# Blocks of 128-token and 64-token experts in turns, fifth place at 64 tokens, largest expert's rest at 32

## The chip, the cores and the metric

The kernel runs on one core of a Trainium2 chip, in one launch. The metric is the device time of one execution in microseconds (us), taken as the median of several runs. TensorE multiplies matrices into PSUM, ScalarE (ACT) and VectorE (DVE) work on tiles, SyncE (SP) issues nearly all transfers from HBM to SBUF, and GpSimd (POOL) does a few small things.

## The reference

Two layers. Each mixes 256 tokens of width 1024 (an RWKV-7 group, an attention group and a gated-MLP group) and then applies a SwiGLU feed-forward: a dense one in layer 0, and in layer 1 the best two of eight experts for each token.

```python
def swiglu(h, wg, wu, wd):
    return (jax.nn.silu(h @ wg) * (h @ wu)) @ wd

def moe_swiglu(h, router, wg, wu, wd):
    t = h.reshape(B_ * S_, D_)                      # 256 x 1024
    logits = (t @ router).astype(jnp.float32)
    top_v, top_i = lax.top_k(logits, TOP_K)         # 2 of 8
    gates = jax.nn.softmax(top_v, axis=-1)
    gate_full = jnp.sum(jax.nn.one_hot(top_i, N_EXPERTS) * gates[..., None], axis=1)
    out = jnp.zeros_like(t)
    for e in range(N_EXPERTS):                      # wg, wu: 1024 x 3584, wd: 3584 x 1024
        out = out + gate_full[:, e:e + 1] * swiglu(t, wg[e], wu[e], wd[e])
    return out
```

All is float32. The change is in the experts alone.

## The kernel before

**Places.** The experts' stage gathers each expert's tokens and computes on those. Expert 0 has place 0; the other seven are sorted by their token count at run time into places 1 (most tokens) to 7. A place has a fixed number of tokens (`KINDS`, `PLACES`, `CAPS`): 128 for places 0, 2, 3 and 4 (wide), 64 for places 5, 6 and 7 (narrow), 128 and a rest of 64 for place 1. If an expert had more tokens than its place, `rest` would compute those at the end, under a condition read at run time, and load the expert's weights again.

**Blocks.** The 3584 hidden columns are cut into seven blocks of 512 (`NB`). A block needs 4 MB of gate and up weights and 2 MB of down weights: six loads of 1 MB (`eload`, lines 1106 and 1108, issued by SP in the order of use) into 12 buffers named raw, which are handed out in turn. Each load is two halves of 1024 columns.

**Wide products.** For 128 tokens a half is split into two reduced-precision parts wh and wl (`split`: ScalarE line 189, VectorE line 190), and each product is three fast ones (`mm3`, lines 194 to 196). A wide block is 72 products of 512 columns: 48 up (into pb), 24 down (into pa). Splits are put two halves ahead of their use (`AHEAD`), into three buffers plus one.

**Narrow products.** For 64 tokens the raw half is used in full precision and not split. The weights' columns are cut in two, and the two products write PSUM rows 0 to 63 and 64 to 127 (`HALF`), so that they use different column halves of the array (line 1437 up, 32 a block; line 1491 down, 8 a block). The profile has two records for each full-precision product.

**Between them.** `gate_up` ends in silu (ScalarE, line 1446) and the product of gate and up (VectorE, line 1449); `act_T` transposes the result (lines 1467 and 1461) and copies it to aT (lines 1470 and 1463); `do_down` multiplies it with the down weights one block later.

**Order.** `SEQUENCE` says which blocks follow each other: places 0, 3 and 2 whole; then pieces of place 1 (two, three and two blocks) with places 7, 6 and 5 whole between them; place 4 last. Place 1's rest goes with its wide blocks and uses the same weights. `halves` supplies the loads and splits in that order; `take` and `fill` keep three halves at hand. `prepare` gathers a place's tokens (lines 1240 and 1254) and `finish` scales an expert's result and adds it back to x (lines 1360, 1361, 1379, 1380); both are cut into steps that are put between the products (`step`). A place that comes in several parts is finished after each part. What comes out is then put in a final order on each engine by a scheduler, so that products of different tiles can stand between each other.

```python
SEQUENCE = ((0, 0, 7), (3, 0, 7), (2, 0, 7), (1, 0, 2), (7, 0, 7), (1, 2, 5), (6, 0, 7), (1, 5, 7), (5, 0, 7), (4, 0, 7))
CAPS = [sum(PLACES[k] for k in KINDS[p]) for p in range(NE)]
```

## Time and profile before

| | us |
|---|---|
| median of 3 runs | 1571.8 (1570.5 to 1573.4) |
| profiled execution, its own time | 1577.0 |
| its span, first to last instruction | 1575.1 |
| span up to the experts' first weight product | 556.5 |

The mean granted TensorE clock is 0.978 of full speed. A row of the timeline gives start and length, engine, line, operation and tiles, out<-in; xN merges N rows of one kind. A row of a group ends in busy time and the mean length in ns, then the engine's idle time just before such instructions and what ended it. A row of a window gives the stretch, its length, the busy time of TensorE, its weight loads, VectorE, ScalarE and GpSimd (with their instructions), the granted clock, the DMA engines' busy share and GB/s. Lengths of products overlap, so the distance of two starts says more than a length.

### The profile page before, as it was taken

What the parts mean: (1) busy time and instruction counts of PE and PEld (TensorE: products, weight loads), DVE (VectorE), ACT (ScalarE), POOL (GpSimd) and SP (SyncE); (2) the same over time, 40 slices, a digit from 0 to 9 for tenths busy, and PEclk for the clock granted to TensorE, in tenths of its full rate; (3) what the DMA queues carried; (4) which work ended last, traced back from release to release, by engine and by line L of the source; (5) the groups of instructions that cost most, each with busy time, mean ns of one, the idle gap of its engine ahead of it and who ended that gap; (6) DMA issues with size and microseconds to landing.
All of it is one profiled execution on the core that took longest, in us unless ns stands there. A gap on an engine that the chain in (4) does not pass through costs nothing.

```text
span 1575.1 us, 24008 instructions
## 1 busy us (share of the span) xinstructions
PE 1530.2 (97%) x9448; PEld 1133.3 (72%) x9448; DVE 941.9 (60%) x1246; ACT 822.9 (52%) x1166; POOL 79.2 (5%) x127
## 2 busy tenths in 40 slices
PE   8988999999988999999999999999999999999997
PEld 7977788888968788888888876555555555555775
DVE  5775654556774578898898876312542044204886
ACT  7565544446555467777777764203341034114774
POOL 1320000001320100000000000000000000000000
PEclk9999999999987889999999999999999999999999
DMA  6500455553514369998998975799848997899990
GB/s 254 186 29 6 183 187 187 187 177 132 186 55 164 118 249 365 369 352 329 370 368 310 360 294 191 272 411 427 354 169 331 425 427 279 336 400 427 426 411 30
DMA packets 59865, 422.57 MB, mean 268 GB/s; under 512 B 7136, under 2 KB 7136, under 8 KB 9824
## 3 DMA queue, kind: packets, MB, share of 16 engines
q1 hardware_dynamic: 59184, 420.03, 69.1%
q8 instruction: 76, 1.25, 0.3%
q10 hardware_dynamic: 560, 0.93, 0.2%
q14 instruction: 45, 0.37, 0.1%
HBM read 419.88 MB, written 1.05 MB: 267 GB/s over the span
## 4 chain that ended last, share of the span: by engine, by line
PE 83%; DMA 3%; DVE 3%; ACT 3%; POOL 2%; issue 1%; ACTq 0%; SPq 0%
PE pb L1437 12%; PE pb L194 11%; PE pb L195 11%; PE pb L196 11%; PE pa L194 7%; PE pa L195 7%; PE pa L196 7%; PE pa L1491 5%; DMA raw<-moe 3%; PE pb L1254 1%; PE pb L1467 1%; PE pb L1240 1%; PE pb L731 1%; POOL rq_y L202 1%; ACT area L964 1%
## 5 line engine op out<-in xcount | busy, mean ns | idle before, releaser
L190 DVE TENSOR_TENSOR wl<-raw,wh 128x1024 fp32r<-128x1024 f32 (+1 forms) x538 | 642.0, 1220 | 246.4 <-ACT wh L189 240.6
L189 ACT ACTIVATE wh<-raw 128x1024 fp32r<-128x1024 f32 (+1 forms) x538 | 559.6, 1055 | 342.9 <-PE pb L196 160.3
L194 PE MATMUL pb<-wh,xg 128*128 128x512 f32 x560 | 226.4, 405 | 1.7 <-ACT wh L189 1.5
L1437 PE MATMUL pb<-raw,xgs 128*64 128x256 f32 x1792 | 227.0, 384 | 0.0
L195 PE MATMUL pb<-wl,xg 128*128 128x512 f32 x560 | 225.7, 403 | 0.3
L196 PE MATMUL pb<-wh,xg 128*128 128x512 f32 x560 | 221.8, 396 | 0.0
L1437 PEld LDWEIGHTS pb<-raw,xgs 128*64 128x64 f32 x1792 | 125.4, 136 | 87.9 <-issue 34.2
L1449 DVE SCALAR_TENSOR_TENSOR a<-pb,rg,a 128x512 f32<-128x512 f32 (+1 forms) x63 | 39.5, 629 | 161.1 <-PE pb L1437 147.8
L194 PEld LDWEIGHTS pb<-wh,xg 128*128 128x128 f32 x560 | 105.9, 189 | 38.9 <-issue 10.0
L195 PEld LDWEIGHTS pb<-wl,xg 128*128 128x128 f32 x560 | 106.1, 189 | 31.4 <-issue 5.8
L196 PEld LDWEIGHTS pb<-wh,xg 128*128 128x128 f32 x560 | 105.9, 189 | 23.1 <-issue 0.5
L1446 ACT ACTIVATE a<-pb,rg 128x512 f32<-128x512 f32 (+1 forms) x63 | 37.3, 593 | 162.2 <-PE pb L1437 137.8
L195 PE MATMUL pa<-wl,aT 128*128 128x512 f32 x280 | 111.6, 399 | 0.0
L196 PE MATMUL pa<-wh,aT 128*128 128x512 f32 x280 | 109.6, 392 | 0.0
L1491 PE MATMUL pa<-raw,aT 128*64 128x512 f32 x448 | 107.8, 599 | 0.0
L194 PE MATMUL pa<-wh,aT 128*128 128x512 f32 x280 | 95.2, 403 | 0.7 <-ACT aT L1470 0.7
L195 PE MATMUL pb<-wl,hTh 128*128 128x512 f32 (+1 forms) x192 | 73.0, 380 | 0.0
L196 PE MATMUL pb<-wh,hTl 128*128 128x512 f32 (+1 forms) x192 | 71.6, 376 | 0.0
L194 PEld LDWEIGHTS pa<-wh,aT 128*128 128x128 f32 x280 | 52.3, 188 | 24.4 <-issue 12.8
L194 PE MATMUL pb<-wh,hTh 128*128 128x512 f32 (+1 forms) x192 | 67.5, 378 | 0.6 <-ACT hTh L277 0.6
L1491 PEld LDWEIGHTS pa<-raw,aT 128*64 128x64 f32 x448 | 30.5, 136 | 48.9 <-issue 45.7
L196 PEld LDWEIGHTS pa<-wh,aT 128*128 128x128 f32 x280 | 52.7, 188 | 10.8
(385 smaller groups left out, 1990.5 us busy)
## 6 DMA issues: line engine op xcount, KB each, us to landing
raw<-moe SPq DMA_DIRECT2D x336, 1024.0 KB, 7.0
raw<-wst SPq DMA_DIRECT2D x54, 1024.0 KB, 4.8
raw<-wst SPq DMA_DIRECT2D x4, 832.0 KB, 5.0
area<-sw_in SPq DMA_DIRECT2D x2, 960.0 KB, 6.7
area<-sw_in SPq DMA_DIRECT2D x2, 664.0 KB, 6.3
x<-x_in SPq DMA_DIRECT2D x2, 512.0 KB, 5.0
raw<-wst SPq DMA_DIRECT2D x2, 512.0 KB, 7.5
out_dram<-x SPq DMA_DIRECT2D x4, 256.0 KB, 3.2
```

The source lines that it names most:

```text
L189: act(h[:, 0:n], t[:, a:b], AF.Copy)
L190: (E or V).tensor_tensor(lo[:, 0:n], t[:, a:b], h[:, 0:n].bitcast(F32), op=ALU.subtract)
L194: T.matmul(o, lhsT=xh, rhs=wh, start=first, stop=False)
L195: T.matmul(o, lhsT=xh, rhs=wl, start=False, stop=False)
L196: T.matmul(o, lhsT=xl, rhs=wh, start=False, stop=last)
L202: G.tensor_tensor(y, m, C("half")[:, 0:n], op=ALU.pow)
L731: T.matmul(ps[HALF[hv], i * 64:(i + 1) * 64], lhsT=lh, rhs=rh, start=(n == 0 and i == 0), stop=(n == len(groups) - 1), skip_group_check=True)
L964: act(s[:, h, :], s[:, h, :], AF.Exp, scale=scale, bias=mx[:, h:h + 1], accum_out=den[:, h:h + 1])
L1437: T.matmul(ps[i][HALF[hv], 0:256], lhsT=z[:, k, :], rhs=w[:, o_:o_ + 256], start=(k == 0), stop=(k == KD - 1))
L1446: act(a[:, 0:m], ps[i][:, 0:m], AF.Silu, scale=r)
L1449: V.scalar_tensor_tensor(res[i][:, 0:m], ps[i][:, 0:m], r, res[i][:, 0:m], op0=ALU.mult, op1=ALU.mult)
L1491: T.matmul(accs[j][0][HALF[nh], :], lhsT=z[:, f, :], rhs=w[:, s_], start=begin, stop=end)
```

## The change

- **Place 4** becomes narrow: 64 tokens in place of 128.
- **Place 1's rest** has 32 tokens in place of 64. Its up and down weights are cut into column quarters: four products of 256 columns write PSUM rows 0 to 31, 32 to 63, 64 to 95 and 96 to 127 (`QUART`, `quarter_up`, `small_down`). They run after the wide block's own products, on the same loads, which stay in their buffers until then.
- **Order.** `SEQUENCE` goes. `work` makes a round for each wide block (places 0, 1, 2, 3 in that order, `WIDES`) and puts one narrow block (places 4, 5, 6, 7, `NARROWS`) into each, none in the first two rounds, two in the 11th and the 20th (`TURNS`). A round is: wide up, quarter up in place 1, wide down of the block before, its quarter down, narrow down of the narrow block before, narrow up.
- **Supply.** `halves` follows the rounds. `fill` counts only split halves, up to two ahead after a `take`, within a window of ten halves.
- **`finish`** has its own buffers (oh, ol) instead of those of the splits, and a form for quarters. Place 1 is finished once.
- **`rest`** computes what exceeds a place in chunks of 64 and 128 tokens.

```diff
-NPT = 4
+NPT = 5
 AHEAD = 2
+WINDOW = 10
...
-WIDE, NARROW = "full", "half"
-PLACES = {WIDE: 128, NARROW: 64}
-KINDS = {0: (WIDE,), 1: (WIDE, NARROW), 2: (WIDE,), 3: (WIDE,), 4: (WIDE,), 5: (NARROW,), 6: (NARROW,), 7: (NARROW,)}
-
-SEQUENCE = ((0, 0, 7), (3, 0, 7), (2, 0, 7), (1, 0, 2), (7, 0, 7), (1, 2, 5), (6, 0, 7), (1, 5, 7), (5, 0, 7), (4, 0, 7))
+WIDE, NARROW, QUARTER = "full", "half", "quarter"
+PLACES = {WIDE: 128, NARROW: 64, QUARTER: 32}
+IOTA = {WIDE: "iota", NARROW: "iota64", QUARTER: "iota32"}
+KINDS = {0: (WIDE,), 1: (WIDE, QUARTER), 2: (WIDE,), 3: (WIDE,), 4: (NARROW,), 5: (NARROW,), 6: (NARROW,), 7: (NARROW,)}
+
+
+WIDES = (0, 1, 2, 3)
+NARROWS = (4, 5, 6, 7)
+
+TURNS = [0, 0] + [2 if _i in (8, 17) else 1 for _i in range(26)]
...
-                    xg.append((kind, late.tile([128, KD, 64], F32, name="xgs", tag="xgs", bufs=3), rs))
+                    w = PLACES[kind]
+                    xg.append((kind, late.tile([128, KD, w], F32, name="xgs", tag="xgs" + kind, bufs=w // 32), rs))
...
+            w = acc[0].shape[-1]
+            parts = (slice(0, 128),) if len(acc) == 2 else HALF if w == 512 else QUART
+            os = []
+            for ps in acc:
+                oh = ap_.tile([128, 512], F32R, name="oh", tag="oh", bufs=2)[:, 0:w]
+                ol = ap_.tile([128, 512], F32R, name="ol", tag="ol", bufs=2)[:, 0:w]
+                act(oh, ps, AF.Identity, scale=sg)
+                V.scalar_tensor_tensor(ol, ps, sg, oh.bitcast(F32), op0=ALU.mult, op1=ALU.subtract)
+                os.append((oh, ol))
...
+            for i in range(DM // w):
+                oh, ol = os[i % len(acc)]
+                rows = parts[i % len(parts)]
+                s_ = slice(i * w, i * w + w)
                 for t in range(2):
-                    ps = pb()
-                    T.matmul(ps, lhsT=pT[:, t * 128:t * 128 + 128], rhs=oh[:, s_], start=True, stop=False)
-                    T.matmul(ps, lhsT=pT[:, t * 128:t * 128 + 128], rhs=ol[:, s_], start=False, stop=True)
+                    ps = pb()[:, 0:w]
+                    lh = pT[rows, t * 128:t * 128 + 128]
+                    T.matmul(ps, lhsT=lh, rhs=oh[rows, :], start=True, stop=False)
+                    T.matmul(ps, lhsT=lh, rhs=ol[rows, :], start=False, stop=True)
...
+        def units(p, i, js):
+            for j in js:
+                r_ = eload(ready[p][0], 6 * i + j)
+                for q in range(2):
+                    a_, b_ = q * 1024, q * 1024 + 1024
+                    if WIDE not in KINDS[p]:
+                        yield None, None, r_[:, a_:b_]
+                    else:
+                        cnt_splits[0] += 1
+                        own = NHL > 0 and cnt_splits[0] % (3 + NHL) < NHL
+                        yield *(split(r_, a_, b_, h2_p, l2_p) if own else split(r_, a_, b_)), r_[:, a_:b_]
+
         def halves():
-            before = None
-            blocks = [(p, i) for p, lo, hi in SEQUENCE for i in range(lo, hi)]
-            for n in range(len(blocks) + 1):
-                for b, js in ((n, range(4)), (n - 1, (4, 5))):
-                    if 0 <= b < len(blocks):
-                        p, i = blocks[b]
-                        whole = KINDS[p] == (NARROW,)
-                        for j in js:
-                            r_ = eload(ready[p][0], 6 * i + j)
-                            for q in range(2):
-                                a_, b_ = q * 1024, q * 1024 + 1024
-                                if whole:
-                                    yield None, None, r_[:, a_:b_]
-                                else:
-                                    cnt_splits[0] += 1
-                                    own = NHL > 0 and cnt_splits[0] % (3 + NHL) < NHL
-                                    yield *(split(r_, a_, b_, h2_p, l2_p) if own else split(r_, a_, b_)), r_[:, a_:b_]
+            m, before = 0, []
+            for n in range(len(wides) + 1):
+                if n < len(wides):
+                    yield from units(*wides[n], range(4))
+                if n > 0:
+                    yield from units(*wides[n - 1], (4, 5))
+                for b in before:
+                    yield from units(*b, (4, 5))
+                before = narrows[m:m + TURNS[n]] if n < len(wides) else []
+                m += len(before)
+                for b in before:
+                    yield from units(*b, range(4))
 
         supply = halves()
         def fill(n=0):
-            while len(feed) <= AHEAD + n:
+            while len(feed) < WINDOW and sum(h[0] is not None for h in feed) <= AHEAD + n:
                 h = next(supply, None)
                 if h is None:
                     break
                 feed.append(h)
 
         def take():
-            fill()
-            return feed.popleft()
-
-        def gate_up(xg, mid):
-            res = []
+            if not feed:
+                fill()
+            h = feed.popleft()
+            fill(-1)
+            return h
...
+        def wide_up(st):
+
+            _, z, rs = st
+            ws = []
+            a = ap_.tile([128, 512], F32, name="a", tag="a0", bufs=2)
             for j in range(2):
-                ps = [pb() for _ in xg]
+                ps = pb()
                 for q in range(4):
                     wh, wl, w = take()
-                    for i, st in enumerate(xg):
-                        for kk in range(2):
-                            k = q * 2 + kk
-                            z = st[1]
-                            if st[0] == WIDE:
-                                s_ = slice(kk * 512, (kk + 1) * 512)
-                                mm3(ps[i], z[:, k, 0, :], z[:, k, 1, :], wh[:, s_], wl[:, s_], k == 0, k == KD - 1)
-                            else:
-                                for hv in range(2):
-                                    o_ = kk * 512 + hv * 256
-                                    T.matmul(ps[i][HALF[hv], 0:256], lhsT=z[:, k, :], rhs=w[:, o_:o_ + 256],
-                                             start=(k == 0), stop=(k == KD - 1))
+                    ws.append(w)
+                    for kk in range(2):
+                        k = q * 2 + kk
+                        s_ = slice(kk * 512, (kk + 1) * 512)
+                        mm3(ps, z[:, k, 0, :], z[:, k, 1, :], wh[:, s_], wl[:, s_], k == 0, k == KD - 1)
...
+        def narrow_up(st):
+
+            _, z, rs = st
+            a = ap_.tile([128, 256], F32, name="a", tag="a1", bufs=2)
+            for j in range(2):
+                ps = pb()[:, 0:256]
+                for q in range(4):
+                    w = take()[2]
+                    for kk in range(2):
+                        k = q * 2 + kk
+                        for hv in range(2):
+                            o_ = kk * 512 + hv * 256
+                            T.matmul(ps[HALF[hv], :], lhsT=z[:, k, :], rhs=w[:, o_:o_ + 256],
+                                     start=(k == 0), stop=(k == KD - 1))
...
+        def quarter_up(st, ws):
+
+            _, z, rs = st
+            a = ap_.tile([128, 256], F32, name="a", tag="a2", bufs=1)
+            ps = pb()[:, 0:256]
+            for k in range(KD):
+                for g in range(4):
+                    o_ = k % 2 * 512 + g % 2 * 256
+                    T.matmul(ps[QUART[g], :], lhsT=z[:, k, :], rhs=ws[g // 2 * 4 + k // 2][:, o_:o_ + 256],
+                             start=(k == 0), stop=(k == KD - 1))
+            act(a[HALF[1], :], ps[HALF[0], :], AF.Silu, scale=rs[1][HALF[0], :])
+            V.scalar_tensor_tensor(a[HALF[1], :], ps[HALF[1], :], rs[1][HALF[1], :], a[HALF[1], :],
+                                   op0=ALU.mult, op1=ALU.mult)
+            return a
...
+        def small_down(acc, kind, i, aT, ws):
+            parts = HALF if kind == NARROW else QUART
+            w = 1024 // len(parts)
+            for f in range(4):
+                for g, rows in enumerate(parts):
+                    T.matmul(acc[rows, :], lhsT=aT[:, f, :], rhs=ws[f][:, g * w:g * w + w],
+                             start=(i == 0 and f == 0), stop=(i == NB - 1 and f == 3))
+
+        def ended(p, kind, acc, final=False):
+
+            (steps.append if final else steps.appendleft)(finish(ready[p][2][KINDS[p].index(kind)], acc, final))
...
+        def work():
+            m, before, wjob = 0, [], None
+            for n in range(len(wides) + 1):
+
+                if wjob is not None:
+                    p, i, a, aq = wjob
+                    aT = wide_T(a)
+                    aqT = small_T(aq, QUARTER, HALF[1]) if aq is not None else None
+                prev, wjob = wjob, None
+                if n < len(wides):
+                    wp, wi = wides[n]
+                    st = ready[wp][1]
+                    a_, ws = wide_up(st[0])
+                    wjob = (wp, wi, a_, quarter_up(st[1], ws) if len(st) > 1 else None)
+                    if wi == 0 and wp != WIDES[-1]:
+                        ask(WIDES[WIDES.index(wp) + 1])
+                    if n == 0:
+                        ask(NARROWS[0])
+                nT = [small_T(a_, NARROW) for _, _, a_ in before]
+                if prev is not None:
+                    ws = wide_down(p, i, aT)
+                    if i == NB - 1:
+                        ended(p, WIDE, accs[p])
+                    if aqT is not None:
+                        if i == 0:
+                            accs[p, QUARTER] = pa()[:, 0:256]
+                        small_down(accs[p, QUARTER], QUARTER, i, aqT, ws)
+                        if i == NB - 1:
+                            ended(p, QUARTER, [accs[p, QUARTER]])
+
+                for (np_, ni, _), z in zip(before, nT):
+                    if ni == 0:
+                        accs[np_] = [pa()]
+                    small_down(accs[np_][0], NARROW, ni, z, [take()[2] for _ in range(4)])
+                    if ni == NB - 1:
+                        ended(np_, NARROW, accs[np_], np_ == NARROWS[-1])
+                new = narrows[m:m + TURNS[n]] if n < len(wides) else []
+                m += len(new)
+                before = []
+                for np_, ni in new:
+                    before.append((np_, ni, narrow_up(ready[np_][1][0])))
+                    if ni == 0 and np_ != NARROWS[-1]:
+                        ask(NARROWS[NARROWS.index(np_) + 1])
...
+                    for kind in (NARROW, WIDE):
+                        if o >= SEQ:
+                            break
+                        here = nc.values_load(over_i[0:1, p:p + 1], min_val=0, max_val=SEQ)
+                        with tc.If(here > o - CAPS[p]):
+                            rest_of(p, kind, o)
```

Three places show what this does to the order. The first is TensorE where narrow and wide blocks meet: pb<-raw,xgs is narrow up, pa<-raw,aT narrow down, pb<-cc,a a transpose, pb<-wh,xg wide up. Before, at the end of the run of place 7:

```order
L1437 MATMUL pb<-raw,xgs 64x256 x24
L1491 MATMUL pa<-raw,aT 64x512 x8
L194 MATMUL pb<-wh,xg 128x512
L1437 MATMUL pb<-raw,xgs 64x256 x8
L1461 MATMUL pb<-cc,a 128x128 x2
L195 MATMUL pb<-wl,xg 128x512
L196 MATMUL pb<-wh,xg 128x512
```

Now, at the end of a round of a late place:

```order
L1531 MATMUL pa<-raw,aT 64x512 x4
L1464 MATMUL pb<-raw,xgs 64x256 x24
L1491 MATMUL pb<-cc,a 128x128 x4
L1464 MATMUL pb<-raw,xgs 64x256 x8
L200 MATMUL pb<-wh,xg 128x512
L201 MATMUL pb<-wl,xg 128x512
L202 MATMUL pb<-wh,xg 128x512
```

Such a change from narrow to wide now comes in every round; the transposes of the wide block before (L1491) stand eight narrow products ahead of the next wide block.

The second is TensorE in place 1. Before, in the block of place 1 that follows place 7 (L1491 here is still place 7's):

```order
L1437 MATMUL pb<-raw,xgs 64x256 x4
L1491 MATMUL pa<-raw,aT 64x512 x8
L194 MATMUL pb<-wh,xg 128x512
L195 MATMUL pb<-wl,xg 128x512
L196 MATMUL pb<-wh,xg 128x512
```

Now, from the end of a wide block's down products to the next wide block (32x256 are the quarters):

```order
L202 MATMUL pa<-wh,aT 128x512
L1531 MATMUL pa<-raw,aT 32x256 x16
L1531 MATMUL pa<-raw,aT 64x512 x8
L1464 MATMUL pb<-raw,xgs 64x256 x32
L1491 MATMUL pb<-cc,a 128x128 x4
L1503 MATMUL pb<-cc,a 128x64 x2
L200 MATMUL pb<-wh,xg 128x512
```

The 16 quarter down products stand together here, with the narrow block behind them and the transposes directly ahead of the wide block; in other rounds of place 1 they are cut by wide products.

The third is ScalarE, where wh<-raw is the first part of a split, a<-pb,rg the silu, and aT<-pb the copy after a transpose (128x4x128 wide, 128x2x2x64 narrow). Before, in a block of place 4:

```order
L189 ACTIVATE wh<-raw 128x1024 x2
L1446 ACTIVATE a<-pb,rg 128x512
L189 ACTIVATE wh<-raw 128x1024 x8
L1470 ACTIVATE aT<-pb 128x4x128
L189 ACTIVATE wh<-raw 128x1024 x4
```

Now, in one round of a late place:

```order
L1494 ACTIVATE aT<-pb 128x4x128
L195 ACTIVATE wh<-raw 128x1024 x7
L1447 ACTIVATE a<-pb,rg 128x512
L195 ACTIVATE wh<-raw 128x1024
L1505 ACTIVATE aT<-pb 128x2x2x64
L195 ACTIVATE wh<-raw 128x1024 x4
L1467 ACTIVATE a<-pb,rg 128x256
```

The copy of the wide aT moved from the middle of the block to its start, behind the narrow silu, and the 12 splits of a block follow it.

221 lines of the change are left out of this document (86 added, 135 removed).

## The prediction

> **What bounds the kernel now.** I read the page's busy shares and its chain of waits first, then windows by stage, then single rows of the experts' stage.
>
> ```profile
> span 1575.1 us, 24008 instructions
> ...
> PE 1530.2 (97%) x9448; PEld 1133.3 (72%) x9448; DVE 941.9 (60%) x1246; ACT 822.9 (52%) x1166; POOL 79.2 (5%) x127
> ...
> PE 83%; DMA 3%; DVE 3%; ACT 3%; POOL 2%; issue 1%; ACTq 0%; SPq 0%
> ```
>
> TensorE is busy 97% of the span and carries 83% of the chain that ended last; transfers carry 3%. So the question is how much TensorE time the change takes out, and whether transfers then become the bound. Only the experts' stage changes. Its first and last weight products are these (timeline, start and length):
>
> ```profile
> 556.53 0.78 PE L194 MATMUL pb<-wh,xg 128*128 128x512 f32 x1
> ...
> 1564.38 0.39 PE L196 MATMUL pa<-wh,aT 128*128 128x512 f32 x1
> ```
>
> The stage is 1564.4 - 556.5 = 1007.9 us. Its unit is a block, 512 hidden columns of one expert. VectorE ends each block's gate and up with one product (L1449), so two of these rows in a steady stretch give the price of a block:
>
> ```profile
> 763.91 0.74 DVE L1449 SCALAR_TENSOR_TENSOR a<-pb,rg,a 128x512 f32<-128x512 f32 x1
> ...
> 815.23 0.74 DVE L1449 SCALAR_TENSOR_TENSOR a<-pb,rg,a 128x512 f32<-128x512 f32 x1
> ...
> 1237.37 0.48 DVE L1449 SCALAR_TENSOR_TENSOR a<-pb,rg,a 128x256 f32<-128x256 f32 x1 [10.38 <-PE pb L1437]
> ...
> 1269.95 0.48 DVE L1449 SCALAR_TENSOR_TENSOR a<-pb,rg,a 128x256 f32<-128x256 f32 x1 [10.38 <-PE pb L1437]
> ...
> 1517.49 0.74 DVE L1449 SCALAR_TENSOR_TENSOR a<-pb,rg,a 128x512 f32<-128x512 f32 x1
> ...
> 1552.82 0.75 DVE L1449 SCALAR_TENSOR_TENSOR a<-pb,rg,a 128x512 f32<-128x512 f32 x1
> ```
>
> Three wide blocks lie between the first two: 51.32 / 3 = **17.11 us**. Three narrow blocks lie between the next two: 32.58 / 3 = **10.86 us**. The last pair, two blocks of place 4, gives 17.67. The program has 35 wide blocks (five places of seven) and 28 narrow ones (21 of places 5 to 7, seven of place 1's rest): 35 x 17.11 + 28 x 10.86 = 598.9 + 304.1 = 903.0 us. The other 104.9 us are gathering, adding back, changes between the two kinds of product, and waits.
>
> Transfers: one block is six loads.
>
> ```profile
> raw<-moe SPq DMA_DIRECT2D x336, 1024.0 KB, 7.0
> ```
>
> ```profile
> 590.00:670.00 80.00, 80.00 (x357) 65.22 (x356) 71.43 (x66) 63.32 (x66) 0.00 (x0) 1.00 0.97 367
> 1085.00:1130.00 45.00, 44.41 (x226) 24.95 (x224) 22.93 (x22) 21.40 (x25) 0.00 (x0) 1.00 1.01 425
> 1445.00:1500.00 55.00, 54.88 (x237) 40.72 (x236) 46.65 (x46) 40.74 (x43) 0.00 (x0) 1.00 1.01 426
> ```
>
> The last three columns are granted clock, DMA share and GB/s. With 12 buffers to refill the queue brings 426 GB/s, while VectorE is 85% busy (46.65 of 55) with splitting. At that rate a block's 6 x 1.0486 MB take 14.8 us: more than a narrow block computes (10.9), less than a wide one (17.1). So a run of seven narrow blocks eats the buffers, and what follows it waits for a while.
>
> **The change, term by term.** Mean splitting costs don't move per block; 84 of 420 splits go, from engines that are not the bound.
>
> *Fifth place, 128 to 64 tokens.* Seven wide blocks go: -7 x 17.11 = **-119.8 us**. Seven narrow blocks come: +7 x 10.86 = +76.0.
>
> *Place 1's rest, 64 to 32 tokens.* Seven narrow blocks go: -76.0, so the narrow count stays 28. Seven quarter blocks come. The chain's pieces of one narrow block price them (start, length, what):
>
> ```profile
> 1226.39 3.43 PE pa L1491 x16
> 1229.83 3.45 PE pb L1437 x32
> 1233.28 0.37 PE pb L1461 x2
> 1233.65 3.60 PE pb L1437 x32
> ```
>
> A full-precision product is two records. Sixteen products of 256 columns take 3.45 us, 0.216 each; eight of 512 take 3.43. That is with the two column halves running together. Whether a quarter product joins three others has no row. From below: four at once, so two pairs' time for four, 0.43. Then 32 up products cost 3.45, 16 down products of 256 columns 1.73, transposes 0.37: 5.5 us a block. From above: no better than two at once, 10.86 us. I count the pieces into which the order of the changed program cuts them, each rounded up to a group of four: 30 pieces up make 69 groups, 17 down 33, so 102 x 0.4315 = 44.0, and with 7 x 0.37 for transposes 46.6 us, 6.7 a block. The row that speaks for this end is the first of these, with its neighbours:
>
> ```profile
> 928.21 0.40 PE L194 MATMUL pb<-wh,xg 128*128 128x512 f32 x1
> 928.54 1.95 PE L1437 MATMUL pb<-raw,xgs 128*64 128x256 f32 x16
> 930.42 0.50 PE L195 MATMUL pa<-wl,aT 128*128 128x512 f32 x1
> ...
> 1099.70 0.39 PE L196 MATMUL pb<-wh,xg 128*128 128x512 f32 x1
> 1100.02 1.08 PE L1437 MATMUL pb<-raw,xgs 128*64 128x256 f32 x6
> 1101.03 0.50 PE L194 MATMUL pb<-wh,xg 128*128 128x512 f32 x1
> 1101.46 0.65 PE L1437 MATMUL pb<-raw,xgs 128*64 128x256 f32 x2
> 1102.04 0.50 PE L195 MATMUL pb<-wl,xg 128*128 128x512 f32 x1
> ```
>
> One product alone holds the array 0.58 us (1101.46 to 1102.04), eight hold it 1.88 (928.54 to 930.42), where eight alone would be 4.6: pairs lose nothing, so groups are independent, and I take **+47 us**.
>
> The Trainium skill, page "TensorE: Matmul & The Clock Gate", Part 3 (Packing small matmuls), measured 3.07 times for four row tiles and 2.38 for three column tiles, not 4 and 3. By it, as an estimate, the 44.0 would be 57, and the total 13 us higher, inside my range; for two halves this trace shows no such loss.
>
> *Interruptions.* In the rows above, entering a narrow piece takes 0.32 where wide products follow each other at 0.23 (763.81 to 764.04 below), and the eight products take 1.88 instead of 8 x 0.216 = 1.73: together 0.25 us a piece. A piece with an odd count also leaves half a group empty (0.2 to 0.4).
>
> ```profile
> 763.81 0.39 PE L195 MATMUL pa<-wl,aT 128*128 128x512 f32 x1
> 764.04 0.39 PE L196 MATMUL pa<-wh,aT 128*128 128x512 f32 x1
> ```
>
> The order has 166 such pieces before (42 odd) and 150 now (47 of them quarters; 20 of the other 103 odd): -16 x 0.25, and 42 x 0.216 against 10 x 0.216 + 10 x 0.43: **-6 us** (0 to -10).
>
> *Adding back and gathering.* Place 1 was finished three times, since its run came in three parts; now once.
>
> ```profile
> L1379 PE MATMUL pb<-oh,pT 128*128 128x512 f32 x28 | 11.9, 442 | 0.3 <-ACT oh L1371 0.3
> ...
> L1380 PE MATMUL pb<-ol,pT 128*128 128x512 f32 x28 | 10.7, 400 | 0.0
> ...
> L1360 PE MATMUL pb<-oh,pT 64*128 64x512 f32 x24 | 9.6, 466 | 0.0
> L1361 PE MATMUL pb<-ol,pT 64*128 64x512 f32 x24 | 8.4, 402 | 0.0
> ```
>
> 104 products become 80 (16 of them half as wide). Between their spacing of wide products (0.23) and busy time per product (11.9 / 28 = 0.43) I take 0.3: **-7 us** (-5 to -10). Gathering (L1254, L1240) stays: one wide turns narrow, a few us at most.
>
> *Waits.* They move both ways. The stages after narrow runs show idle TensorE:
>
> ```profile
> 1432.00:1565.00 133.00, 131.68 (x570) 99.29 (x566) 109.55 (x103) 93.28 (x101) 0.00 (x0) 1.00 0.78 328
> ```
>
> 1.3 us here, 0.6 in the 1085 window, and place 4's 17.67 against 17.11 for its later blocks: some 5 us, hidden waits unseen. Against it, every round now starts a wide block behind a narrow one. In place 4's block the copy of aT stands on ScalarE ahead of the next splits and waits for the transposes; that is the 0.56. In the new order two splits are ahead, and in most rounds the transposes stand eight narrow products (1.7 us) ahead of the wide block's first, which covers the copy; where they stand directly ahead (place 1's rounds) I count 0.56 each. Sum **0** (-12 if waits of the mixed stages were larger than seen, +15 if all 27 rounds pay 0.56).
>
> What is late next? Six loads of a wide and six of a narrow block take 2 x 14.8 = 29.5 us. A round's TensorE time is 17.11 + 10.86 plus a share of the rest, (104.9 - 13) / 28 = 3.3: 31.3 us, in place 1 some 38. So transfers stay just under, and two wide rounds at the start fill the buffers first. SP issues all loads in the order of use. In place 1 four of the 12 buffers stay taken until the quarter products at the block's end, and the loads behind them on SP wait; eight loads then stand ready, 19.7 us of transfer, for the down and narrow products of some 18 us that come first. The two rounds with two narrow blocks need 44.3 us of loads against 42 and draw on 12 buffers.
>
> *Tail.* The last wide place is now added back together with the last narrow one. These rows end the kernel:
>
> ```profile
> 1565.07 1.41 DVE L1372 SCALAR_TENSOR_TENSOR ol<-pa,sg,oh 128x512 fp32r<-128x512 f32 x2 [2.75 <-ACT oh L1371]
> 1566.67 2.48 DVE L1381 TENSOR_TENSOR x<-x,pb 128x512 f32<-128x512 f32 x4 [0.19 <-PE pb L1380]
> ```
>
> Both stand once more, 3.9 us, partly beside the narrow down products (3.43): **+1.5** (0 to +4).
>
> Sum: -119.8 + 47 - 6 - 7 + 0 + 1.5 = -84.3 us. The profiled execution itself took 1577.0 (span 1575.1), so it would be 1492.7; the runs' median is 1571.8, and -84.3 gives **1487 us**. The layers before are re-ordered in a few rows only (and one constant is 64 KB longer): 3 us either way.
>
> **Rivals.**
>
> *Quarters no better than halves.* If both passes of a product must leave before the next group's first, four groups run two at a time: 7 x 10.86 = 76 instead of 47, so 1487 + 29 = 1516. For it: no row has four groups. Against it: in the 928.54 piece eight products take eight times 0.216 plus entry and exit (1.88), with no ninth slot. The Trainium skill, the same page and part, calls products strict FIFO in start and end; by that rule the queue would run this way, and the piece's 1.88 us does not bear it out for two groups.
>
> *Transfers become the bound.* The 590 window has the queue 97% busy at only 367 GB/s while wide blocks run. Were that the most that splitting leaves, 324 loads after the first 12 would take 339.7 MB / 367 = 926 us from 556.5, to 1482; the last narrow block and the tail add about 16: some 1500 as a span, 1497 by the median, up to 1515 with uneven rounds. Against it: the 1445 window, 426 GB/s beside as much splitting; 367 is what 17.11 us blocks ask for (6.29 MB / 17.11 = 368).
>
> *Splits late in every round.* With none ahead, a round would pay copy, split and subtraction, 0.59 + 1.06 + 1.22 = 2.9 us; 27 rounds make 78, so 1565. The durations are those of the rows below.
>
> ```profile
> L190 DVE TENSOR_TENSOR wl<-raw,wh 128x1024 fp32r<-128x1024 f32 (+1 forms) x538 | 642.0, 1220 | 246.4 <-ACT wh L189 240.6
> L189 ACT ACTIVATE wh<-raw 128x1024 fp32r<-128x1024 f32 (+1 forms) x538 | 559.6, 1055 | 342.9 <-PE pb L196 160.3
> ...
> L1470 ACT ACTIVATE aT<-pb 128x512 fp32r<-128x512 f32 x35 | 20.5, 587 | 10.9 <-PE pb L1467 8.4 <-PE pa L196 2.2
> ```
>
> *Slower: the overflow path runs.* From the 65th token of the fifth-fullest place, or the 161st of the fullest, 42 loads and a narrow expert follow alone at the end: 42 x 2.46 = 103 us of loads and some 10 to gather and add: 1600. The reference on its inputs gives 16 tokens to expert 0 and, in order, 147, 120, 70, 55, 54, 36, 14: nine and 13 short of it.
>
> **How the numbers follow.** Forecast 0.68, quarters 0.13, transfers 0.11, late splits 0.05, overflow 0.02, else 0.01. The range: all low bounds together (5.5 a quarter block, -12 waits, -10, -10, no tail) give 1455; they won't all fall together, so 1460. Above, it takes in the first two rivals with the high bound of the waits: 1525. Late splits and overflow stay out. 0.2% (3 us) is what a measurement can tell from no change; faster 0.96, same 0.01, slower 0.03.
>
> **What would show it.** In the changed profile: narrow products in 28 blocks spread over the whole stage, L1449's successors 31 us apart; groups of four 32-column records starting together every 0.216 us; DMA share near 0.95 without long waits of TensorE for loads. Wrong would be: quarter pieces at twice that length, TensorE idle at a round's start by over 1 us, or a DMA rate stuck at 370 with TensorE waiting.

## The result, and the profile after

The changed kernel takes **1525.1 us** (median of 4 runs, 1524.0 to 1528.1), the kernel before on the same chip 1571.2 (1569.1 to 1573.4): ratio 0.971, 95% interval 0.9689 to 0.973. It is faster by 46 us. The forecast was 1487, 84 us faster, and the range ended at 1525: the direction was right, the size was little more than half.

The page of the changed kernel, span, TensorE's busy time, the chain's shares by engine, and one of the costliest groups:

```profile
span 1526.2 us, 23806 instructions
...
PE 1463.4 (96%) x9578; PEld 1056.8 (69%) x9578; DVE 820.5 (54%) x1136; ACT 719.8 (47%) x1073; POOL 80.5 (5%) x127
...
PE 81%; DVE 6%; ACT 3%; POOL 2%; issue 2%; DMA 1%; ACTq 0%; DVEq 0%; POOLq 0%
...
L201 PE MATMUL pb<-wl,xg 128*128 128x512 f32 x448 | 185.4, 414 | 12.9 <-DVE wl L196 12.3
```

Transfers went from 3% to 1% of the chain, so they did not become the bound. VectorE went from 3% to 6%, and the last row says where: TensorE stood idle for 12.9 us ahead of the second product of a wide tile, which reads wl (L201, L195 before), and VectorE's split ended nearly all of it.

The first and last products of the experts' stage (timeline):

```profile
568.72 0.78 PE L200 MATMUL pb<-wh,xg 128*128 128x512 f32 x1
...
1517.58 0.39 PE L1379 MATMUL pb<-ol,pT 64*128 64x512 f32 x1
```

The stage begins 12.2 us later than before (556.5), though nothing was changed ahead of it. From its first weight product to the last product of all, 948.9 us pass where it was 1010.4 (556.5 to 1566.9): 61.5 less. 61.5 - 12.2, and 0.4 more behind the last product, make the 48.9 us between the two spans. (The profiled execution of the kernel before took 1577.0, 5 us over its median, so by the medians, 46.1 us apart, the layers ahead cost some 15.) So there are two questions: why the layers ahead got longer, and what the stage lacks of its 84 us.

Quarters first, since they were the unknown price. Three pieces of quarter products (L1480), with what follows each (timeline):

```profile
776.90 0.62 PE L1480 MATMUL pb<-raw,xgs 128*32 128x256 f32 x2
777.45 0.50 PE L200 MATMUL pb<-wh,xg 128*128 128x512 f32 x1
777.87 0.64 PE L1480 MATMUL pb<-raw,xgs 128*32 128x256 f32 x8
778.44 0.50 PE L201 MATMUL pb<-wl,xg 128*128 128x512 f32 x1
...
813.92 1.91 PE L1480 MATMUL pb<-raw,xgs 128*32 128x256 f32 x26
815.76 0.50 PE L201 MATMUL pb<-wl,xg 128*128 128x512 f32 x1
```

Two records are one product. From the start of a piece to the start of what follows it, one product holds the array for 0.55 us, four for 0.57 and thirteen for 1.84. That is 0.4315 for each group of up to four and 0.12 for the piece: 0.55, 0.55 and 1.85. Two at once, thirteen would need 7 x 0.4315 = 3.02. **Four quarters do run together.** By distance of starts they take 33.6 us up, 16.4 down and 2.0 for transposes: 52.0, or 7.4 a block where 6.7 was forecast.

### The profile page after: what moved, and what is told of

It is laid out like the page before. It is cut to its first block, busy times and chain, and to the rows that moved or that the text cites. A ratio compares the mean times of both kernels' runs of the same rounds, so it can differ in the third digit from the quotient of the medians.

```text
span 1526.2 us, 23806 instructions
## 1 busy us (share of the span) xinstructions
PE 1463.4 (96%) x9578; PEld 1056.8 (69%) x9578; DVE 820.5 (54%) x1136; ACT 719.8 (47%) x1073; POOL 80.5 (5%) x127
## 4 chain that ended last, share of the span: by engine, by line
PE 81%; DVE 6%; ACT 3%; POOL 2%; issue 2%; DMA 1%; ACTq 0%; DVEq 0%; POOLq 0%
PE pb L1464 12%; PE pb L201 10%; PE pb L200 9%; PE pb L202 9%; PE pa L1531 8%; PE pa L201 7%; PE pa L200 6%; PE pa L202 6%; PE pb L1480 2%; DVE wl L196 2%; DMA raw<-moe 1%; PE pb L1262 1%; PE pb L1491 1%; PE pb L1248 1%; POOL rq_y L208 1%
## 5 line engine op out<-in xcount | busy, mean ns | idle before, releaser
L196 DVE TENSOR_TENSOR wl<-raw,wh 128x1024 fp32r<-128x1024 f32 (+1 forms) x454 | 541.6, 1219 | 282.4 <-ACT wh L195 277.3
L195 ACT ACTIVATE wh<-raw 128x1024 fp32r<-128x1024 f32 (+1 forms) x454 | 467.2, 1053 | 276.1 <-PE pb L202 159.6
L201 PE MATMUL pb<-wl,xg 128*128 128x512 f32 x448 | 185.4, 414 | 12.9 <-DVE wl L196 12.3
L200 PE MATMUL pb<-wh,xg 128*128 128x512 f32 x448 | 181.6, 407 | 0.0
L202 PE MATMUL pb<-wh,xg 128*128 128x512 f32 x448 | 177.9, 397 | 0.0
L1531 PE MATMUL pa<-raw,aT 128*64 128x512 f32 (+1 forms) x672 | 128.3, 530 | 0.0
L201 PEld LDWEIGHTS pb<-wl,xg 128*128 128x128 f32 x448 | 85.1, 190 | 49.1 <-DVE wl L196 23.9
L1495 DVE TENSOR_TENSOR aT<-pb,aT 128x512 fp32r<-128x512 f32 x28 | 19.3, 690 | 180.5 <-ACT aT L1494 180.5
L200 PEld LDWEIGHTS pb<-wh,xg 128*128 128x128 f32 x448 | 85.1, 190 | 24.7 <-ACT wh L195 5.0
L202 PEld LDWEIGHTS pb<-wh,xg 128*128 128x128 f32 x448 | 85.0, 190 | 16.5
L201 PE MATMUL pa<-wl,aT 128*128 128x512 f32 x224 | 92.4, 413 | 0.2 <-DVE wl L196 0.2
L202 PE MATMUL pa<-wh,aT 128*128 128x512 f32 x224 | 88.3, 394 | 0.0
L1531 PEld LDWEIGHTS pa<-raw,aT 128*64 128x64 f32 (+1 forms) x672 | 35.8, 127 | 65.4 <-issue 60.0
L200 PE MATMUL pa<-wh,aT 128*128 128x512 f32 x224 | 77.5, 405 | 0.0
L201 PE MATMUL pb<-wl,hTh 128*128 128x512 f32 (+1 forms) x192 | 73.0, 380 | 0.0
L201 PEld LDWEIGHTS pa<-wl,aT 128*128 128x128 f32 x224 | 42.1, 188 | 30.2 <-issue 20.2
L200 PE MATMUL pa<-wh,hTh 128*128 128x512 f32 (+1 forms) x128 | 50.1, 406 | 3.9 <-ACT hTh L763 2.8
```

The costliest lines, as they stand in the source:

```text
L195: act(h[:, 0:n], t[:, a:b], AF.Copy)
L196: (E or V).tensor_tensor(lo[:, 0:n], t[:, a:b], h[:, 0:n].bitcast(F32), op=ALU.subtract)
L200: T.matmul(o, lhsT=xh, rhs=wh, start=first, stop=False)
L201: T.matmul(o, lhsT=xh, rhs=wl, start=False, stop=False)
L202: T.matmul(o, lhsT=xl, rhs=wh, start=False, stop=last)
L1495: V.tensor_tensor(z[:, :, 1, :], p3, z[:, :, 0, :].bitcast(F32), op=ALU.subtract)
```

## Experiments

Each kernel ran in three rounds beside the kernel before; its ratio is to those runs. This table has the profiled executions (us; the stage from its first weight product to the last product):

| kernel | median | ratio, interval | stage begins | stage length |
|---|---|---|---|---|
| before | 1571.2 | 1 | 556.5 | 1010.4 |
| changed | 1525.1 | 0.971 (0.9689 to 0.973) | 568.7 | 948.9 |
| b_const | 1586.6 | 1.007 (1.0036 to 1.0104) | 564.9 | 1011.0 |
| a_noconst | 1511.0 | 0.9597 (0.9566 to 0.9627) | 552.5 | 948.7 |
| a_split | 1511.4 | 0.9609 (0.9582 to 0.9636) | 564.7 | 934.8 |
| a_both | 1496.2 | 0.9515 (0.9487 to 0.9544) | 546.2 | 934.7 |
| s_act | 1531.9 | 0.9756 (0.973 to 0.9782) | 564.8 | 954.3 |
| s_dve | 1525.1 | 0.9696 (0.9676 to 0.9717) | 564.7 | 949.8 |
| q_half | 1526.0 | 0.9705 (0.9689 to 0.9721) | 550.6 | 963.0 |
| q_none | 1438.0 | 0.9137 (0.9115 to 0.916) | 550.6 | 875.6 |
| o_narrow | 1547.6 | 0.9831 (0.9808 to 0.9855) | 559.5 | 983.1 |
| t_wide | 1537.2 | 0.9782 (0.9754 to 0.981) | 552.1 | 978.2 |
| t_wide2 | 1538.3 | 0.9796 (0.9776 to 0.9815) | 547.0 | 978.4 |
| w_two | 1417.1 | 0.9027 (0.8998 to 0.9057) | 546.6 | 857.0 |

Where two kernels have the same stage, its length agrees within 0.6 us (changed and a_noconst, a_split and a_both, before and b_const). Its beginning scatters by up to 13 us among kernels with the same work ahead. So the stage's terms are read from lengths.

### The layers ahead of the experts

On VectorE, ahead of layer 0's output products, the kernel before has this order (timeline; L747 is a part of the RWKV group's result, L445 the addition to x):

```profile
160.26 1.45 DVE L747 TENSOR_TENSOR shp<-ysb,rq_y 64x192 f32<-64x192 f32 x4 [1.75 <-POOL rq_y L202]
...
164.12 0.55 DVE L754 TENSOR_TENSOR zv<-pb,zv 128x384 f32<-128x384 f32 x1
...
165.92 0.69 DVE L445 TENSOR_TENSOR x<-x,pa 128x512 f32<-128x512 f32 x1 [0.66 <-PE pa L196]
```

In the changed kernel the same lines (now L754, L761, L451) stand in another order; VectorE's rows, then TensorE's:

```profile
167.87 1.28 DVE L451 TENSOR_TENSOR x<-x,pa 128x512 f32<-128x512 f32 x2 [1.39 <-PE pa L202]
169.07 1.45 DVE L754 TENSOR_TENSOR shp<-ysb,rq_y 64x192 f32<-64x192 f32 x4
171.22 0.56 DVE L761 TENSOR_TENSOR zv<-pb,zv 128x384 f32<-128x384 f32 x1 [0.70 <-PE pb L758]
```

```profile
170.66 0.52 PE L758 MATMUL pb<-cc,shp 128*128 128x128 f32 x3 [1.13 <-DVE shp L754]
172.98 0.79 PE L200 MATMUL pa<-wh,hTh 128*128 128x512 f32 x1 [1.80 <-ACT hTh L763]
173.57 0.63 PE L201 MATMUL pa<-wl,hTh 128*128 128x512 f32 x1
174.00 0.63 PE L200 MATMUL pa<-wh,hTh 128*128 128x512 f32 x1
```

The additions wait for TensorE, the RWKV result waits behind them, and TensorE has nothing else left. What then comes runs at 0.43 us a product in place of 0.23. The windows before, in and after that wait (the last three columns are granted clock, DMA share and GB/s):

```profile
160.00:167.80 7.80, 7.80 (x42) 5.86 (x41) 2.91 (x3) 2.86 (x4) 1.15 (x2) 1.00 0.58 202
168.00:173.00 5.00, 1.50 (x8) 0.61 (x6) 3.63 (x9) 0.52 (x1) 0.20 (x1) 0.93 0.43 179
173.00:179.00 6.00, 6.00 (x14) 4.74 (x15) 1.74 (x2) 1.55 (x2) 0.00 (x0) 0.50 0.00 0
```

The granted clock is 0.50 for 6 us after a stretch of 5 us in which TensorE was busy for 1.5. Products that ran 1.5 us later than before at 142 us run 9.5 us later at 181. The Trainium skill, page "TensorE: Matmul & The Clock Gate", Part 1, has the array fall to half its clock after about 3.4 us of idle time. Here the longest single wait was 1.80 us, with a few short products between, and the clock fell as well.

What moved the order? The one thing that the change adds ahead of the experts is a longer constant. b_const adds it to the kernel before; a_noconst takes it from the changed kernel (of each edit the main line).

```diff
-... ("iota64", 128), ("caps", 8), ...
+... ("iota64", 128), ("iota32", 128), ("caps", 8), ...
```

> The kernel before with one thing of the change alone: the constant of 128 more columns, which nothing reads here. Theory (the longer constant alone makes the scheduler place layer 0's work differently, and that is the 12.2 us by which the first wide product of the experts starts later): slower by 9 to 13 us, about 1583, with the first wide product near 568.7 us and the shift coming up between 140 and 185 us, where layer 0's shifted sums on VectorE stand behind the additions to x. Rival (the later start comes from the change in the experts, whose first loads and gathers are traced earlier): within 2 us of before, first wide product near 556.5.

```diff
-                i = V.tensor_scalar(d[:, t, :], C("iota32"), float(o + 1), sl, ...)
+                i = V.tensor_scalar(d[:, t, :].rearrange("p (g s) -> p g s", g=4),
+                                    C("iota")[:, None, 0:32].to_broadcast([128, 4, 32]), float(o + 1), sl, ...)
```

> The changed kernel without the extra constant: the one-hot of the 32-token part reads the first 32 columns of the old constant four times over. Theory (layers' order): the layers go back to the order of before, the first wide product to about 556.5 us, the time to 1511 to 1517. Rival: within 2 us of the changed kernel's 1525.

Measured: b_const 1586.6 against 1572.3 for the kernel before on its chip, slower with an interval of 6 to 16 us; its stage begins at 564.9 (568.7 expected) and has its old length. a_noconst takes 1511.0, 14 us under the changed kernel. Over all runs the stage begins at 564.7 to 568.7 with the long constant (five kernels) and at 546.2 to 559.5 without (nine). The constant's own transfer is not what is late: at 134 us the two kernels are still level. VectorE's 583 instructions ahead of the stage stand in one order in all nine kernels without the long constant and in one other order in all five with it. **The theory holds: 64 KB more in a constant gave another order ahead of the experts and cost some 14 us.**

The 14 us come up in two places, not in one. In layer 0, between the same two products (at 151.0 and 173.9 us in the kernel before), the nine kernels take 22.9 us each and the five 30.8 or 30.9, with 4.0 us of idle TensorE in place of 0.5 and a clock of 0.50 from about 172 to 179 us that none of the nine has. In layer 1 the output products come once more, and the additions and the splits swap again. Between the same two products there (at 498.1 and 535.0 in a_noconst, 318 products) the five take 42.7 to 43.1 us and seven of the nine 36.5 to 36.9. (The other two, the kernel before and o_narrow, take 42.7 and 42.8, with the clock at 0.50 for 17 us of it.) TensorE's waits there in the changed kernel:

```profile
540.95 0.74 PE L200 MATMUL pa<-wh,hTh 128*128 128x512 f32 x2 [1.15 <-ACT wh L195]
542.57 0.50 PE L201 MATMUL pa<-wl,hTh 128*128 128x512 f32 x1 [0.88 <-DVE wl L196]
546.28 0.50 PE L200 MATMUL pa<-wh,hTh 128*128 128x512 f32 x1 [0.96 <-ACT hTh L763]
```

That the swapped additions are the rows that do it is read from the trace; they were not put back alone, and splits of wl moved with them.

### The late splits

In eight rounds from 1183 us on, the first and second product of a wide block stand 1.79 us apart with nothing between them. (In five more, the first at 1079 us, the distance is the same, but products that add back or gather fill part or all of it.) One of the eight, rows of TensorE, ScalarE and VectorE:

```profile
1438.50 0.65 PE L1491 MATMUL pb<-cc,a 128*128 128x128 f32 x4
...
1439.08 1.95 PE L1464 MATMUL pb<-raw,xgs 128*64 128x256 f32 x16
1439.19 0.60 ACT L1494 ACTIVATE aT<-pb 128x512 fp32r<-128x512 f32 x1 [1.83 <-PE pb L1491]
1439.68 3.89 ACT L195 ACTIVATE wh<-raw 128x1024 fp32r<-128x1024 f32 x4
1439.82 0.69 DVE L1495 TENSOR_TENSOR aT<-pb,aT 128x512 fp32r<-128x512 f32 x1 [12.48 <-ACT aT L1494]
...
1440.96 0.49 PE L200 MATMUL pb<-wh,xg 128*128 128x512 f32 x1
1441.08 0.48 DVE L1469 SCALAR_TENSOR_TENSOR a<-pb,rg,a 128x256 f32<-128x256 f32 x1 [0.57 <-PE pb L1464]
1441.48 2.35 DVE L196 TENSOR_TENSOR wl<-raw,wh 128x1024 fp32r<-128x1024 f32 x2
...
1442.75 0.50 PE L201 MATMUL pb<-wl,xg 128*128 128x512 f32 x1 [1.29 <-DVE wl L196]
```

VectorE idles for 12.48 us, then does L1495 (waits for the wide transposes) and L1469 (waits for the last narrow product), and only then the first wl, which TensorE needs at once. ScalarE likewise makes no wh until its copy L1494 is through. Eight such waits are 8 x 1.56 = 12.5 us over the usual 0.23; smaller ones in other rounds make up to 15.

a_split makes the copy and the activation stand behind the newest split, and so behind the one before it too, on both engines; s_act and s_dve do it on one engine each. `newest` holds the two instructions of the split made last.

```diff
+            with tc.issue_after(newest[0].ins), tc.issue_after(newest[1].ins):
                 act(z[:, :, 0, :], p3, AF.Copy)
                 V.tensor_tensor(z[:, :, 1, :], p3, z[:, :, 0, :].bitcast(F32), op=ALU.subtract)
...
+                    with tc.issue_after(newest[1].ins):
                         V.scalar_tensor_tensor(a, ps, rs[0], a, op0=ALU.mult, op1=ALU.mult)
```

> The changed kernel with one thing more: on ScalarE and VectorE the first two splits of the next wide block stand ahead of the last narrow activation and of the copy of the wide transposes, which in the changed kernel stand ahead of them in 8 late rounds. Theory (late splits): the eight waits of 1.79 us between the first product and the second go to 0.23, and the smaller ones of 0.2 to 0.7 us too, together 12 to 15 us: about 1512. Rival one (transfers): the waits go, but 12 loads a round take 29.5 us where a round now takes 30.3, so at most 0.8 us a round comes back, 6 us in all: about 1519. Rival two (the wait is the change of tile shape and not the split): the gap stays at 1.79 us and the time within 2 us of 1525.

> Both edits together: no extra constant, splits ahead. If the two causes are separate, the gains add up: 12 and 13 us, about 1500. If the transfers bind once TensorE waits less, 1505 to 1507. If neither cause holds, 1525.

> Run a_split with its edit on ScalarE alone: the first two high parts of the next wide block stand ahead of the copy of the wide transposes, while VectorE keeps the last narrow activation ahead of their low parts. Theory (the wait is VectorE's order: a low part behind an activation that waits for the end of the narrow products): the late gaps between first and second product stay at 1.79 us and the time at the changed kernel's 1525, ratio 0.971. Rival (ScalarE's order makes the wait): the gaps go, about 1511, ratio 0.961.

> Run a_split with its edit on VectorE alone: the low parts stand ahead of the last narrow activation, but ScalarE makes the first high part only behind the copy of the wide transposes (from 1439.68 us on in the round of the changed kernel in which the first product starts at 1440.96). High part 1.05 us, low part 1.22 us: the low part is there about 1 us after the first product. Theory (both engines' orders count, one behind the other): late gaps of 1.0 to 1.1 us, 8 x 0.7 = 6 us of the 14 come back, about 1519, ratio 0.967. If VectorE's order is all of it: 1511, 0.961.

Measured: a_split 1511.4, and its stage is 14.1 us shorter: the theory, not the two rivals. Its wide blocks start level with the changed kernel's up to the 19th (1183 us there), and all 14.1 us come behind. Its late rounds take 28.7 us where they took 30.3. That is under the 29.5 that their 12 loads take at 427 GB/s, so the buffers give the rest. TensorE's waits for wl in the stage (view of waits: us in total, times, longest), the changed kernel and then a_split:

```profile
PE pb L201 <- DVE wl L196: 12.3, 13, 1.3
```

```profile
PE pb L204 <- DVE wl L198: 1.5, 5, 0.5
```

VectorE's rows of a_both at such a place:

```profile
1463.22 2.36 DVE L198 TENSOR_TENSOR wl<-raw,wh 128x1024 fp32r<-128x1024 f32 x2 [11.41 <-ACT wh L197]
1465.96 0.48 DVE L1478 SCALAR_TENSOR_TENSOR a<-pb,rg,a 128x256 f32<-128x256 f32 x1 [0.38 <-PE pb L1472]
```

Both low parts now stand ahead of the narrow activation. a_both takes **1496.2 us**, 15 us under either edit alone: the causes are separate, and this version beats both kernels (1491 to 1498 in its runs).

With one engine's order mended, a wait stays. Rows of s_act, then s_dve:

```profile
1438.14 1.04 ACT L197 ACTIVATE wh<-raw 128x1024 fp32r<-128x1024 f32 x1
...
1440.90 0.49 PE L203 MATMUL pb<-wh,xg 128*128 128x512 f32 x1
1441.08 0.48 DVE L1472 SCALAR_TENSOR_TENSOR a<-pb,rg,a 128x256 f32<-128x256 f32 x1 [13.83 <-PE pb L1467]
1441.49 2.35 DVE L198 TENSOR_TENSOR wl<-raw,wh 128x1024 fp32r<-128x1024 f32 x2
1442.76 0.51 PE L204 MATMUL pb<-wl,xg 128*128 128x512 f32 x1 [1.36 <-DVE wl L198]
```

```profile
1436.17 4.88 ACT L197 ACTIVATE wh<-raw 128x1024 fp32r<-128x1024 f32 x5
1437.25 2.36 DVE L198 TENSOR_TENSOR wl<-raw,wh 128x1024 fp32r<-128x1024 f32 x2 [13.43 <-ACT wh L197]
1437.45 0.49 PE L203 MATMUL pb<-wh,xg 128*128 128x512 f32 x1
1438.53 0.50 PE L204 MATMUL pb<-wl,xg 128*128 128x512 f32 x1 [0.59 <-DVE wl L198]
```

In s_act the high part is there at 1439.2 and helps nothing: 1.86 us, as VectorE's order demands. It was even slower than the 1525 expected, 1531.9, and its stage is 5.4 us longer than the changed kernel's; 3.4 of these are more idle time of TensorE (19.6 us in the stage for 16.2), the rest was not found. In s_dve VectorE is free and waits for ScalarE: 1.08 us, as worked out. The waits for wl in s_dve:

```profile
PE pb L204 <- DVE wl L198: 8.6, 23, 0.6
```

Half as long a wait came nearly twice as often: in each of the eight rounds a second one, of 0.2 us, follows. The 6 us expected of s_dve did not come: its stage is 949.8 long, 0.9 more than the changed kernel's. By the starts of the wide blocks it gains 2.5 us from the 16th to the 28th and has lost 2.8 before, 2.4 of them in one round of place 1 (40.3 us from 963.9 on, where the changed kernel takes 37.9). What makes that round longer was not found. Only both orders together bring the 14 us.

### The prices in the new order

q_half gives place 1's rest halves again (its products and transposes take that form too), q_none leaves it out (`CAPS` stays, so `rest` does not run), t_wide and t_wide2 make the fifth place wide, all on a_both; o_narrow makes it narrow in the kernel before; w_two takes a third of TensorE's wide work in the experts away.

```diff
-KINDS = {..., 1: (WIDE, QUARTER), ...}
+KINDS = {..., 1: (WIDE, NARROW), ...}
```

> Run a_both (no extra constant, splits ahead; 1496 us, 0.9515 of before) with the 19 tokens of the largest expert's rest in 64 columns and halves in place of 32 and quarters, as the kernel before has them, in the new turns. A narrow block takes 10.86 us of TensorE before; the quarters' groups of rows of the changed kernel add up to 52 us for 7 blocks, 7.4 each. Theory (four quarters run at once): slower by 7 x 3.4 = 24 us, about 1520, ratio 0.967. Rival (quarters are no better than halves): 1496, ratio 0.9515.

```diff
-KINDS = {..., 1: (WIDE, QUARTER), ...}
+KINDS = {..., 1: (WIDE,), ...}
```

> Run a_both with place 1's rest left out: the 19 tokens beyond 128 of the largest expert get nothing from it. This prices the quarters whole. By the rows of the changed kernel's trace (33.6 + 16.4 + 2.0 us of TensorE): faster than a_both by 52 us, about 1444, ratio 0.918. By the 6.7 us a block of the prediction: by 47 us, 1449. If their work lay partly under waits, by less than 40: 1456 or more.

```diff
-KINDS = {..., 4: (WIDE,), ...}
+KINDS = {..., 4: (NARROW,), ...}
```

> The kernel before with the fifth place narrow and nothing else: its seven blocks stand at the end behind the seven of the sixth place, 14 narrow blocks in a row. TensorE alone would save 7 x (17.11 - 10.86) = 44 us: 1528, ratio 0.972. Theory (without turns the loads bind): 14 blocks need 84 loads of 2.45 us, 206 us, where TensorE needs 152; twelve buffers full at the start carry 29 us of the 54: so 20 us are saved at most and 10 if the buffers are not full, 1552 to 1562, ratio 0.987 to 0.994.

```diff
-KINDS = {..., 4: (NARROW,), ...}
+KINDS = {..., 4: (WIDE,), ...}
-WIDES = (0, 1, 2, 3)
-NARROWS = (4, 5, 6, 7)
-TURNS = [0, 0] + [2 if _i in (8, 17) else 1 for _i in range(26)]
+WIDES = (0, 1, 2, 3, 4)
+NARROWS = (5, 6, 7)
+TURNS = [0, 0] + [0 if _i % 3 == 2 else 1 for _i in range(31)] + [0, 0]
```

> Run a_both with the fifth place wide again: 35 wide blocks and 21 narrow, which stand in two of three rounds. Theory (the fifth place's part of the gain is 7 x (17.11 - 10.86) = 44 us once the loads keep up): 1540, ratio 0.979. If the turns themselves cost (each change between wide and narrow), seven narrow blocks fewer save that too, and it comes out nearer 1532. If the loads bound a_both, less is lost: 1525 or below.

```diff
-                    ended(np_, NARROW, accs[np_], np_ == NARROWS[-1])
+                    ended(np_, NARROW, accs[np_])
-                        ended(p, WIDE, accs[p])
+                        ended(p, WIDE, accs[p], p == WIDES[-1])
```

> Run t_wide once more with its stores moved: in t_wide the last narrow place's stores went out before the last wide place's additions, so its end lacked them. With the stores behind the last wide place: within 6 us of t_wide's 1537, ratio 0.978 to 0.982, so that the fifth place is worth 41 to 47 us in the new turns (predicted: 44).

```diff
         T.matmul(o, lhsT=xh, rhs=wh, start=first, stop=False)
-        T.matmul(o, lhsT=xh, rhs=wl, start=False, stop=False)
-        T.matmul(o, lhsT=xl, rhs=wh, start=False, stop=last)
+        T.matmul(o, lhsT=xh, rhs=wl, start=False, stop=last)
```

> Run a_both with the third of the three products of every wide tile left out in the experts (low part of the tokens by high part of the weights), which takes 2016/3 x 0.2305 = 155 us from TensorE and nothing from the loads. It shows where the loads bind. By TensorE alone 1496 - 155 = 1341. Theory (a load of 1 MB lands every 2.45 us at best, so a round cannot be under 29.4 us): 13 of 336 loads have landed when the first wide product starts at 546, the other 323 take 791 us, and the last is followed by some 29 us of work: 1366 to 1380. If the loads were what sets a_both's time: about 1490.

Measured, by stage length against a_both's 934.7:

- **q_half** +28.3 (24 expected): quarters instead of halves gain what the forecast said, 76 - 47 = 29.
- **q_none** -59.1 (52 or 47 expected). 53.0 of it are the quarters' own rows in a_both, by distance of starts; wide products take 4.4 more beside them, adding back, gathering and transposes 4.9 more, and narrow products 3.2 less.
- **t_wide2** +43.7, and t_wide +43.5 (44 expected). By rows (distance of starts), t_wide2 has 119.2 more of wide products and 70.1 less of narrow ones, and 5.4 less of the rest.
- **o_narrow** -27.3 against the kernel before's stage, 24.5 by the medians: better than the 10 to 20 expected, and still 16 short of 43.7. Its end shows why (two windows, and TensorE's narrow products from 1390 us on):

```profile
1390.00:1480.00 90.00, 86.04 (x617) 44.40 (x618) 7.27 (x15) 7.00 (x17) 0.00 (x0) 1.00 1.01 420
1480.00:1545.00 65.00, 51.38 (x336) 23.72 (x334) 4.93 (x9) 4.42 (x10) 0.00 (x0) 1.00 0.90 378
```

```profile
L1437 PE MATMUL pb<-raw,xgs 128*64 128x256 f32 x704 | 83.2, 383 | 8.9 <-DMA raw<-moe 6.3 <-ACT a L1446 2.4
```

  In the first window the queue is full (DMA share 1.01), and TensorE waits for loads. In turns the same block is worth its whole price.
- **w_two** 1417.1, where 1341 would be TensorE alone and 1366 to 1380 was expected. Loads are 13% of its chain, and these windows show them at their rate and under it:

```profile
800.00:900.00 100.00, 96.94 (x679) 55.52 (x679) 39.73 (x47) 36.15 (x49) 0.00 (x0) 0.97 0.87 358
...
1200.00:1300.00 100.00, 90.76 (x495) 52.19 (x491) 53.70 (x57) 45.24 (x54) 0.00 (x0) 0.98 1.01 427
```

  The estimate let the queue run at 427 GB/s throughout; in place 1's rounds it brings 358, since there TensorE still has more to do than the queue. These seven rounds last 264 us (704.1 to 968.3, starts of wide blocks) with 8.5 us of idle TensorE, and their 90 loads take 220 at 2.45 each: the 44 us that the estimate lacks. So the loads don't set a_both's time, but they are near in its late rounds (28.7 us each, 29.5 of loads):

```profile
1300.00:1400.00 100.00, 99.02 (x527) 65.67 (x527) 53.80 (x54) 43.79 (x50) 0.00 (x0) 1.00 1.01 426
```

## Why the prediction fell short, step by step

The stage's account, from the lengths above:

| term | forecast | measured | from |
|---|---|---|---|
| fifth place, wide to narrow | -43.8 | -43.7 | t_wide2, a_both |
| place 1's rest, half to quarter | -29.0 | -28.3 | q_half, a_both |
| pieces, adding back, tail, other waits | -11.5 | -3.7 | remainder |
| late splits | 0 | +14.2 | changed, a_both |
| stage | -84.3 | -61.5 | before, changed |
| layers ahead | 0 | +12.2 | first weight products |

- **Fifth place and quarters: right, with some luck.** Both differences are within 0.7 us. The quarter's own price was too low, 59.1 in place of 47, but so was the half's: 28.3 + 59.1 = 87.4 for the 76.0 of 7 x 10.86, and the two errors cancel. What a part costs in entries, gathering and adding back was in neither. In the fifth place the wide blocks were priced right (119.8 for 119.2), the narrow ones 5.9 too high, and 5.4 of other rows make up for that.
- **Waits: the step that failed in the stage.** "In the new order two splits are ahead": on ScalarE and VectorE there were none in eight rounds; the splits stood behind a copy and an activation that wait for TensorE. The third order listing ahead of the prediction already has ScalarE's copy (L1494) in front of seven splits. The prediction looked at the copy on ScalarE and not at VectorE, where the narrow activation (L1469) is the later of the two. Its bound of +15 for the waits came near by chance: it was 27 rounds of 0.56. Its rival of late splits in every round had 2.9 us for each of 27; it was 1.56 in eight.
- **The layers: the other failed step.** "The layers before are re-ordered in a few rows only (and one constant is 64 KB longer): 3 us either way" counted rows and did not ask what waits at them. The swap put additions that wait for TensorE ahead of results that TensorE waits for, once in each layer: 7.9 us in layer 0 and some 6 in layer 1.
- **Rivals.** Quarters no better than halves: fell (1.84 us for 13 products). The quarters' products took 33.6 + 16.4 = 50.0 us where 44.0 was forecast; the 6.0 more are about 0.13 for each of the 47 pieces. By the loss that the Trainium skill's page "TensorE: Matmul & The Clock Gate", Part 3, gives for four row tiles (3.07 times in place of 4), an estimate is 57. The trace does not bear that out. Transfers: fell for this kernel (1% of the chain), true for the end of o_narrow and the late rounds of w_two. Overflow did not run (336 loads, as before).
- With both failed steps undone, a_both is at 1496, 9 us above the forecast: about 8 us in the third row of the table. Adding back, one part of that row, came out as forecast: its products take 28.6 us before and 21.9 in a_both, by distance of starts. The rest of the row was not taken apart.

## What to carry to other kernels

When a change alters what a scheduler sees, read on every engine what stands directly ahead of the work that the busiest engine needs next, and what that waits for; a single row ahead of it can cost more than a count of moved rows suggests, and an unread constant can move it, in layers that the change does not touch. Price two parts by the difference of two runs that have everything else alike: differences held to 1 us here, while the single prices were 11 to 12 us too low and their errors cancelled. Alternating blocks that load longer than they compute with blocks that compute longer keeps both busy, and what it is worth shows only beside a run without the turns.

## What the runs showed of the hardware that was not expected

- Full-precision products of 256 columns on four groups of 32 columns of the array run together without a loss that grows with their number: one holds it 0.55 us, four 0.57, thirteen 1.84, which is 0.43 for each group of four and 0.12 for the piece.
- TensorE's clock fell to 0.50 without any single long wait: TensorE had 1.5 us of work in the 5 us ahead (168 to 173, longest wait 1.80), and the clock stayed low for 6.8 us (172.3 to 179.1), 3.4 us of loss on top of the waits. All five kernels with the long constant show it there, none of the other nine does. How much work would have kept the clock up was not tried.
- The time up to the experts varied by 13 us between executions of kernels with the same order of VectorE's instructions ahead of them (546.2 to 559.5), while the experts' stage repeated within 0.6 us. The clock goes with it: it was 0.50 for 44 to 71 us of that time, and less half of these the nine begin within 5.1 us of each other (521.1 to 526.2).
